# A two-layer hybrid decoder trunk on one core: one plain feed-forward block fewer, zeros set on another engine, and a mended order at the heads

## The chip, the core and the metric

The kernel runs on one core of a Trainium2 chip. Its engines work side by side, each through its own list in order: TensorE (PE; its weight loads are PEld), VectorE (DVE), ScalarE (ACT), GpSimd (POOL), and SyncE (SP), whose queue starts most DMA transfers. The metric is the device time in microseconds (us). Three runs of the kernel before gave a median of 1268.68 us.

## The reference

There are two layers. Each normalises its input, projects it to all heads at once, runs eight forgetting-attention heads and four retention heads, projects their joined outputs back and adds them; then a SwiGLU feed-forward block is added. Sixteen learned tokens stand ahead of the 512 real ones, so layer 0 works on 528 columns.

```
def rmsnorm(x, g):
    y = x32 * lax.rsqrt(jnp.mean(x32 * x32, axis=-1, keepdims=True) + EPS)
...
logit[t,s] = q_t.k_s/sqrt(Dh) + c[t] - c[s], c = cumsum(log f), s <= t     # attention, 8 heads of 64
o_t = sum_{s<=t} gamma_h^(t-s) (q_t.k_s) v_s                               # retention, 4 heads of 128
...
h = h + (silu(x @ w_gate) * (x @ w_up)) @ w_down                           # x: normalised h; 1024 -> 2816 -> 1024
```

## The kernel before

Activations are kept transposed: `h[k]`, k = 0 to 7, holds 128 of the 1024 features over the T = 528 columns. Layer 0 computes all columns in two pieces of 264 (FULL); layer 1 needs the last 512 only (REAL), in one piece.

**Three matmuls for one product.** Each fp32 operand is split into a high part, rounded to the fast matmul's type (`whi`, `xh`, names ending in h or hi), and the rest (`wlo`, `xl`); a product is high times high, high times low, low times high. So each weight tile costs a cast on ScalarE (L199, in the feed-forward's units L900) and a subtraction on VectorE or, in parts of 128, on GpSimd (L202, L901). The same holds for activations (L150 and L151; L327 and L328 for the normalised input). `convert(j)` does it for job j; the job in hand converts the next one's two halves at its second and fifth chunk. `whi` and `wlo` have two buffers.

**Order.** TensorE's order is written out in the program: a list of steps, into which `merge` and `spread` put the steps of the attention heads (`fox_steps`) and the retention heads (`ret_places`) at given positions. The other engines' order is chosen by a scheduler that knows three hints: `high_priority`, `issue_after`, and `pin` (keep in program order). PSUM has four single banks (`psa`) and two double ones (`psd`).

**Attention and retention.** L524 makes a block of logits from the keys with the forget terms (`kc`, built in L467 and L472, and `kx`) and the queries (`qo`, `qs`); L528 masks it and takes the maximum `nmax`, L541 the exponential `pr`; L427 transposes it, and its high and low parts `pth`, `ptl` (L151) go into L586 and L594 against the values. A retention head takes its product in L727, multiplies it by its decay (L732, `sd`), splits it into `rsh` and `rsl`, multiplies by the values in L761 and normalises the head. L664 starts the gate's silu, for heads 0 and 1, with a maximum of x and -80, written as an instruction that takes x twice.

**The feed-forward.** 22 blocks of 128 hidden features go through six rounds, `ROUNDS = ((0, 3), (3, 7), ...)`. A block below PLAIN is plain: gate and up are ordinary products over eight chunks each (96 matmuls of 264 columns in layer 0, 48 of 512 in layer 1), then `u_done` multiplies and splits the result into `ah`, `al`. Any other block is a `Unit`, which makes its two outputs from seven smaller products of half the depth and half the columns, as in fast matrix multiplication: 84 matmuls of 264 columns, in layer 1 of 256. Its parts are a head (first product pair, w1, with the ordinary x), a middle (w2 twice, w3) and a tail (w3, w4). Weights w2, w3, w4 are sums and differences of gate and up weights, formed on VectorE (`make2` to `make4`: L946, L947, L953, L959) and then split: w2 into `fwhi`, `fwlo` from `S` for the first unit of a layer, w3 into `whi`, `wlo` from `fraw`. The x forms (`th`, `tl`, from `S`) are sums of x blocks that `x_forms(0)` to `x_forms(3)` make, inserted every nine steps in the plain blocks. `done` turns a unit's banks into its `ah`, `al`. The products with w_down (`down`, L1047) of a round are put among the units of the next one. The squares for the second norm are summed on VectorE (`ss`, L348), split (`sql`) and summed over partitions by L298.

The final norm's last squares are made in L1140 and summed in L1143 and L1169.

Of the kernel before, what the change touches and what calls it, by code (L numbers as in the profile page):

```python
# [27 lines left out]
PLAIN = 3  # L28
# [11 lines left out]
def hybrid_kernel(ctx, tc, x_t, w_in, w_fl, w_out, w_gate, w_up, w_down, vecs, b_fg, rope, decay, mask, ident, out_t):  # L40
# [42 lines left out]
    def enter_att(l):  # L83
# [37 lines left out]
    def zero(l, t):  # L121
        (nc.gpsimd if l else nc.vector).memset(t, 0.0)  # L122
# [82 lines left out]
    def dense_steps(src, parts, pool=False, banks=False, ahead=(1, 4), own=None, wait=None):  # L205
# [6 lines left out]
        def chunk(k0, k, n, xs, cols, ps, done):  # L212
            def go():
# [77 lines left out]
    def col_rstd(parts, n, cols, rname, pinned=False):  # L291
# [23 lines left out]
    def pin(f, pinned=True):  # L315
        if pinned:
            tc.keep_in_program_order(f)

    def scale_split(st, gcol, cols, then=None):
# [3 lines left out]
        for k in range(NK):  # L323
# [3 lines left out]
            pin(nc.scalar.activation(xh[:, c], h[k][:, c], AF.Copy, scale=g), then)  # L327
# [48 lines left out]
    def forget_gates(l, st):  # L376
# [16 lines left out]
        for ps, (c0, c1) in zip(psf, FULL):  # L393
            with ExitStack() if l else tc.high_priority():
                nc.scalar.copy(z2[:, c0:c1], ps[32:32 + FH, 0:c1 - c0])
# [233 lines left out]
    def ret_dense(l, hd, ly, real, st, which):  # L629
# [23 lines left out]
        def g_done(ps):  # L653
# [3 lines left out]
            if hd > 1:  # L657
                silu(sv(sg, real), LOGS)
# [5 lines left out]
            nc.vector.scalar_tensor_tensor(u, x, -80.0, x, ALU.max, ALU.max)  # L664
# [11 lines left out]
    def ret_steps(l, hd, st, real):  # L676
# [27 lines left out]
        def scores(grp):  # L704
# [87 lines left out]
        def head_norm():  # L792
            d = st["d"]
            r = col_rstd(st["parts"], 128, QC, "r")
# [23 lines left out]
    def out_proj(l, rnd, mix, real):  # L818
# [4 lines left out]
                                rnd == 0 or m2 < 2, rnd == 1 and m2 == 1) for m2 in range(NK // 2)], [])  # L823

    def ffn(l, st, real, last):
# [40 lines left out]
        def x_forms(k):  # L866
            def go():
# [5 lines left out]
                nc.scalar.activation(s[:, 0:2], two(h[k]), AF.Copy, scale=g0)  # L873
# [567 lines left out]
```

## Time and profile before

| | |
|---|---|
| median of three runs | 1268.68 us (1268.33 to 1268.9) |
| profiled execution, its span | 1268.51 us, 1266.7 us |
| granted TensorE clock, mean | 0.998 |
| PE, PEld | 1250.7 us (99%), 1192.2 us (94%) |
| DVE, ACT, POOL | 994.4 us (79%), 706.2 us (56%), 274.3 us (22%) |
| DMA | 116.19 MB, 92 GB/s over the span |
| layer 0's feed-forward, first plain product to first unit | 286.85 to 322.34 us |
| the same in layer 1 | 910.03 to 944.66 us |

In the profile's rows the first number is the start, the second the duration, both in us; then come engine, line, operation, output<-inputs, and xcount where equal neighbours are merged. Square brackets give the idle time before an instruction and who ended it. In rows of waits, the waiting engine and line stand left of the arrow.

### The profile page before, as it was taken

The page shows a single profiled execution, that of the slowest core. Times are in us where ns is not written, and L with a number is a line of the kernel's source. Part 1 is how long each engine was busy: PE and PEld are TensorE (multiplying, and loading weights), DVE is VectorE, ACT ScalarE, POOL GpSimd, SP SyncE. Part 2 cuts the span into 40 slices and gives each one's busy share as a digit, 9 for nine tenths or more (in the row PEclk, how much of TensorE's full clock was granted, in tenths as well). Part 3 has the DMA queues.
Part 4 walks back from the last instruction along what each step waited for, and adds up shares of the span by engine and source line. Part 5 has one row for each costly group of instructions (what it writes and reads, how often), then busy time and mean ns, then how long its engine had stood idle before and what let it go on. Part 6 is the DMA issues. An engine that isn't in the chain of part 4 may idle for free.

```text
span 1266.7 us, 23528 instructions
## 1 busy us (share of the span) xinstructions
PE 1250.7 (99%) x9223; PEld 1192.2 (94%) x9223; DVE 994.4 (79%) x1800; ACT 706.2 (56%) x1305; POOL 274.3 (22%) x540
## 2 busy tenths in 40 slices
PE   9999999999999999999999999999999999999997
PEld 9999999999999999999999989998789999999996
DVE  8887756879988888887786877567899888888867
ACT  7767655676444444444466665557764444444445
POOL 3555546420000000000126556554100000000000
PEclk9999999999999999999999999999999999999999
DMA  6212222223333333332322122222233333333321
GB/s 218 67 60 69 83 76 73 71 67 117 105 97 100 100 101 100 101 101 84 101 77 84 61 84 74 71 89 67 100 96 121 100 101 101 100 101 101 100 84 67
DMA packets 43342, 116.19 MB, mean 92 GB/s; under 512 B 5088, under 2 KB 12000, under 8 KB 43232
## 3 DMA queue, kind: packets, MB, share of 16 engines
q1 hardware_dynamic: 42800, 114.41, 28.1%
q8 instruction: 72, 1.18, 0.4%
q14 instruction: 38, 0.31, 0.1%
q10 hardware_dynamic: 432, 0.29, 0.1%
HBM read 112.58 MB, written 2.10 MB: 91 GB/s over the span
## 4 chain that ended last, share of the span: by engine, by line
PE 91%; DVE 4%; ACT 4%; issue 1%; DMA 0%; ACTq 0%; DVEq 0%
PE psd L225 28%; PE psa L912 18%; PE psd L1047 14%; PE psd L912 13%; PE psa L225 5%; PE psa L1047 4%; PE psa L427 2%; PE psa L524 1%; PE psa L594 1%; PE psa L761 1%; PE psa L727 1%; ACT whi L199 1%; PE psa L298 0%; ACT xh L327 0%; DMA raw<-w_in 0%
## 5 line engine op out<-in xcount | busy, mean ns | idle before, releaser
L202 POOL TENSOR_TENSOR wlo<-raw,whi 128x128 fp32r<-128x128 f32 x504 | 259.1, 548 | 256.0 <-ACT whi L199 235.3
L225 PE MATMUL psd<-xh,whi 128*128 128x264 f32 (+1 forms) x792 | 195.5, 314 | 0.0
L225 PE MATMUL psd<-xh,wlo 128*128 128x264 f32 (+1 forms) x792 | 186.9, 304 | 0.0
L225 PE MATMUL psd<-xl,whi 128*128 128x264 f32 (+1 forms) x792 | 186.4, 303 | 0.4 <-DVE xl L328 0.4
L225 PEld LDWEIGHTS psd<-xh,whi 128*128 128x128 f32 x792 | 128.5, 190 | 4.9 <-ACT whi L199 0.5
L225 PEld LDWEIGHTS psd<-xh,wlo 128*128 128x128 f32 x792 | 127.0, 188 | 6.3 <-DVE wlo L202 0.4
L225 PEld LDWEIGHTS psd<-xl,whi 128*128 128x128 f32 x792 | 127.6, 189 | 5.1 <-DVE xl L328 1.1
L199 ACT CAST whi<-raw 128x512 fp32r<-128x512 f32 (+1 forms) x168 | 97.9, 613 | 41.7 <-PE psd L225 28.6
L900 ACT CAST whi<-raw 128x1024 fp32r<-128x1024 f32 (+2 forms) x62 | 54.8, 885 | 51.2 <-PE psd L912 39.8
L900 ACT CAST fwhi<-raw 128x1024 fp32r<-128x1024 f32 (+2 forms) x62 | 55.6, 897 | 48.0 <-PE psd L912 40.5
L122 POOL MEMSET kc<- 64x528 f32 x2 | 1.1, 532 | 345.4 <-PE psa L912 345.4
L901 DVE TENSOR_TENSOR wlo<-raw,whi 128x1024 fp32r<-128x1024 f32 (+2 forms) x62 | 62.9, 1015 | 12.6 <-ACT whi L900 12.5
L901 DVE TENSOR_TENSOR fwlo<-raw,fwhi 128x1024 fp32r<-128x1024 f32 (+2 forms) x62 | 64.0, 1033 | 11.0 <-ACT fwhi L900 10.7
L912 PE MATMUL psa<-th,whi 128*128 128x264 f32 (+1 forms) x232 | 65.4, 282 | 0.0
L912 PE MATMUL psa<-th,wlo 128*128 128x264 f32 (+1 forms) x232 | 65.4, 282 | 0.0
L912 PE MATMUL psa<-tl,whi 128*128 128x264 f32 (+1 forms) x232 | 65.3, 282 | 0.0
L912 PE MATMUL psa<-th,fwhi 128*128 128x264 f32 (+1 forms) x224 | 63.4, 283 | 0.0
L912 PE MATMUL psa<-tl,fwhi 128*128 128x264 f32 (+1 forms) x224 | 63.3, 283 | 0.0
L912 PE MATMUL psa<-th,fwlo 128*128 128x264 f32 (+1 forms) x224 | 63.2, 282 | 0.0
L541 ACT ACTIVATE pr<-pr,nmax 128x144 f32<-128x144 f32 (+1 forms) x64 | 36.8, 575 | 44.4 <-DVE nmax L528 25.7
L900 ACT CAST fwhi<-S 128x1024 fp32r<-128x1024 f32 x20 | 21.0, 1049 | 68.6 <-PE psa L912 66.5
L978 ACT COPY e<-psa 128x264 f32<-128x264 f32 (+1 forms) x114 | 42.9, 376 | 28.3 <-PE psa L912 24.1
(368 smaller groups left out, 4044.8 us busy)
## 6 DMA issues: line engine op xcount, KB each, us to landing
raw<-w_in SPq DMA_DIRECT2D x54, 512.0 KB, 3.5
raw<-w_gate SPq DMA_DIRECT2D x44, 512.0 KB, 4.0
fraw<-w_up SPq DMA_DIRECT2D x38, 512.0 KB, 3.5
raw<-w_down SPq DMA_DIRECT2D x64, 256.0 KB, 2.9
raw<-w_out SPq DMA_DIRECT2D x16, 512.0 KB, 3.5
raw<-w_down SPq DMA_DIRECT2D x32, 192.0 KB, 2.5
raw<-w_up SPq DMA_DIRECT2D x6, 512.0 KB, 3.5
h<-x_t SPq DMA_DIRECT2D x8, 264.0 KB, 4.5
```

What stands on the lines that cost most here:

```text
L199: pin(nc.scalar.copy(hi, job["raw"][:, c0:c1]), pinned)
L202: pin(sub(lo[:, c:c + step], job["raw"][:, c0 + c:c0 + c + step], hi[:, c:c + step].bitcast(F32)), pinned)
L225: nc.tensor.matmul(ps[1][b][:, 0:c1 - c0], w[:, wk, :], x[:, c0:c1], start=(k == 0 and i == 0), stop=(k == n - 1 and i == 2))
L427: nc.tensor.transpose(ps[:, 128 * j:128 * j + 128], src[:, o:o + 128], idt)
L524: nc.tensor.matmul(sc[0:nq, 0:c1 - c0], qq[:, q0:q0 + nq], kk[:, c0:c1], start=(i == 0), stop=(i == 1))
L541: nc.scalar.activation(pr, pr, AF.Exp, bias=nmax[0:nq], scale=-1.0, accum_out=rsum)
L594: nc.tensor.matmul(po[:, c0:SEQ], v[:, j, :], pp[:, j, META + c0:T], start=(j == 0 and i == 0), stop=(j == 4))
L900: nc.scalar.copy(hi, src)
L901: nc.vector.tensor_sub(lo, src, hi.bitcast(F32))
L912: nc.tensor.matmul(bank()[:, 0:b.shape[-1]], a[:, o + k, :], b, start=(fresh and k == 0 and i == 0), stop=(k == n - 1 and i == 2), skip_gr ...
L978: nc.scalar.copy(self.t["e"][:, i], self.t["x"][:, 0:w])
L1047: nc.tensor.matmul(v[:, 0:c1 - c0], a[:, s * n + k, :], b[:, c0:c1], start=(k == 0 and i == 0), stop=(k == n - 1 and i == 2))
```

## The change

- PLAIN goes from 3 to 2 in both layers: block 2 becomes a unit, still in the first round. With no down products to fill in, its tail follows the next unit's head. The x forms are inserted every seven steps. `whi` and `wlo` get a third buffer, and the gate of block 0 and the last job of the output projection (`far=True`) convert the job after the next one too.
- Layer 0's zeros and ones of the attention's tiles are set on GpSimd.
- The maximum at L664 becomes a `tensor_scalar_max`, with x once.
- In layer 0 the copy of the forget gate's second part is issued after the sum of squares' rounding. The first activation of the x forms in layer 1 is issued after the last xh. Head 2's silu is issued after head 3's last rounding, which has high priority. `rsh` and `rsl` have three buffers. In layer 0 the sums for head 2's norm are copied aside to SBUF, which frees their banks. Some places of the first heads are moved.
- The final norm keeps the square of row 5 as a third tile, so one VectorE sum goes, and the sum over partitions takes four parts, not three.

```diff
-PLAIN = 3
+PLAIN = 2
...
-            (nc.gpsimd if l else nc.vector).memset(q_tiles[s][rest].bitcast(F32), 1.0)
+            nc.gpsimd.memset(q_tiles[s][rest].bitcast(F32), 1.0)
...
-        (nc.gpsimd if l else nc.vector).memset(t, 0.0)
+        nc.gpsimd.memset(t, 0.0)
...
-        return pool.tile([128, NK, 128], F32R, name=tag, tag=tag, bufs=2)
+        return pool.tile([128, NK, 128], F32R, name=tag, tag=tag, bufs=2 if tag[0] == "f" else 3)
...
-                [(NK, *[wp.tile([128, NK, 128], F32R, name=i, tag=i) for i in ("whi", "wlo")])]
+                [(NK, *[wring(i) for i in ("whi", "wlo")])]
...
                 for half, at_step in enumerate(ahead):
                     if k0 + k == at_step:
                         convert(j + 1, 4 * half + 4)
+                        if far:
+                            convert(j + 2, 4 * half + 4)
...
+            if aside:
+                t = tt("sq")
+                for v, (c0, c1) in zip(views, cols):
+                    nc.scalar.copy(t[:, c0:c1], v)
+                views, cols = [t[:, c_all]], [(cols[0][0], cols[-1][1])]
...
-                silu(sv(sg, real), LOGS)
+                with tc.issue_after(other["rounded"]) if hd == 2 else ExitStack():
+                    silu(sv(sg, real), LOGS)
...
-            nc.vector.scalar_tensor_tensor(u, x, -80.0, x, ALU.max, ALU.max)
+            nc.vector.tensor_scalar_max(u, x, -80.0)
...
-            sh = at("rsh", bufs=2)
-            sl = at("rsl", bufs=2)
+            sh = at("rsh", bufs=3)
+            sl = at("rsl", bufs=3)
...
-            split(sh[:, 0:full], sl[:, 0:full], sd[:, 0:full])
+            with tc.high_priority() if hd == RH - 1 and grp[0] == 2 else ExitStack():
+                st["rounded"] = nc.scalar.copy(sh[:, 0:full], sd[:, 0:full]).ins
+                nc.vector.tensor_sub(sl[:, 0:full], sd[:, 0:full], sh[:, 0:full].bitcast(F32))
...
-                                rnd == 0 or m2 < 2, rnd == 1 and m2 == 1) for m2 in range(NK // 2)], [])
+                                rnd == 0 or m2 < 2, rnd == 1 and m2 == 1, far=rnd == 1 and m2 == 3) for m2 in range(NK // 2)], [])
...
-                nc.scalar.activation(s[:, 0:2], two(h[k]), AF.Copy, scale=g0)
+                with tc.issue_after(st["scaled"].ins) if real else ExitStack():
+                    nc.scalar.activation(s[:, 0:2], two(h[k]), AF.Copy, scale=g0)
...
-                    steps += dense_steps(w_gate[l, f], [(0, xs, NK, QC, g_done(f) if f else held.append)], banks=f == 1)
+                    steps += dense_steps(w_gate[l, f], [(0, xs, NK, QC, g_done(f) if f else held.append)], banks=f == 1, far=f == 0)
...
             def after_7():
                 square_b(7)
-                sum_b(5)
                 v = psum_a()[:, 0:nb]
-                sums(v, [fin["one"][0], fin["acc"], fin["one"][1]])
+                sums(v, [fin["one"][0], fin["acc"]] + fin["one"][1:])
...
-            steps.insert(NK + 4 + 9 * i, x_forms(i))
+            steps.insert(NK + 4 + 7 * i, x_forms(i))
...
-            m0, r0, places = (((7 if l else 11, 31 if l else 32.5), (34, 40.5), (13, 33.5, 35.5, 37.5, 39, 40.5, 43, 44, 47.5, 48)),
+            m0, r0, places = (((7 if l else 12, 31 if l else 33), (34, 40.5), (13 if l else 17.5, 33.5, 35.5, 38.3 if l else 38.6, 39, 40.5, 43, 44, 47.5, 48)),
...
-                      ret_places(3, 52, 45.5, 47.5, 57.5, 55.5, 58.5, 60, 64.1, 63, 64.2))
+                      ret_places(3, 52, 45.5, 47.5, 57.5, 54.9, 58.5, 60, 64.1, 63, 64.2))
```

The first place is VectorE in layer 0's first attention block, around the maximum for silu (L664, now L681; `ge<-sg`). Before:

```order
L655 SCALAR_TENSOR_TENSOR sg<-psd,R 128x528
L528 ISA pr,nmax<-psa,msk 128x264
L528 ISA nmax 128x1
L528 ISA pr,nmax<-psa,msk 128x264
L528 ISA nmax 128x1
L664 SCALAR_TENSOR_TENSOR ge<-sg 128x528
L533 TENSOR_TENSOR nmax<-nmax 128x1
L151 TENSOR_TENSOR ptl<-psa,pth 128x128
```

And now:

```order
L544 ISA pr,nmax<-psa,msk 128x264
L544 ISA nmax 128x1
L544 ISA pr,nmax<-psa,msk 128x264
L544 ISA nmax 128x1
L671 SCALAR_TENSOR_TENSOR sg<-psd,R 128x528
L549 TENSOR_TENSOR nmax<-nmax 128x1
L151 TENSOR_TENSOR ptl<-psa,pth 128x128
L681 TENSOR_SCALAR ge<-sg 128x528
```

The maximum has moved behind `nmax` and the `ptl` for which TensorE's L727 waits. The second place is VectorE at the start of layer 0's feed-forward, around the low part of the first unit's w2 (`fwlo<-S`) and w3 (`wlo<-fraw`). Before, with block 3 as the first unit (`al_4467` is block 1's result):

```order
L151 TENSOR_TENSOR al_4467<-tq,ah_4466 128x528
L946 TENSOR_TENSOR S<-fraw 128x512
L151 TENSOR_TENSOR tl_4286<-S,th_4285 128x1056
L848 SCALAR_TENSOR_TENSOR sg<-psd,R 128x528
L901 TENSOR_TENSOR wlo<-raw,whi 128x1024
L947 TENSOR_TENSOR S<-S,raw 128x512
L953 TENSOR_TENSOR fraw<-raw,fraw 128x512
L959 TENSOR_TENSOR raw<-raw,S 128x512
L901 TENSOR_TENSOR fwlo<-S,fwhi 128x1024
L901 TENSOR_TENSOR fwlo<-raw,fwhi 128x768
L856 SCALAR_TENSOR_TENSOR tq<-psd,R 128x528
L901 TENSOR_TENSOR wlo<-fraw,whi 128x1024
```

And now, with block 2 as the first unit (`al_4477` is block 1's result):

```order
L966 TENSOR_TENSOR S<-fraw 128x512
L897 SCALAR_TENSOR_TENSOR S<-h_80,vec,S 128x264
L875 SCALAR_TENSOR_TENSOR tq<-psd,R 128x528
L967 TENSOR_TENSOR S<-S,raw 128x512
L151 TENSOR_TENSOR tl_4290<-S,th_4289 128x1056
L876 TENSOR_TENSOR tq<-tq,sg 128x528
L921 TENSOR_TENSOR fwlo<-S,fwhi 128x1024
L151 TENSOR_TENSOR al_4477<-tq,ah_4476 128x528
L973 TENSOR_TENSOR fraw<-raw,fraw 128x512
L921 TENSOR_TENSOR fwlo<-raw,fwhi 128x1024
L979 TENSOR_TENSOR raw<-raw,S 128x512
L921 TENSOR_TENSOR wlo<-fraw,whi 128x1024
```

Block 1's result and the forms of w3 and w4 have moved behind w2's low part, and the low part of the next unit's w1 (`fwlo<-raw`, 1024) stands ahead of w3's. The third place is a little later on VectorE, at the end of the first unit's `done`; now it reads:

```order
L921 TENSOR_TENSOR wlo<-S,whi 128x1024
L1013 SCALAR_TENSOR_TENSOR tq<-sg,R 128x528
L921 TENSOR_TENSOR fwlo<-raw,fwhi 128x1024
L1001 TENSOR_TENSOR e<-psd,e 128x264
L1015 TENSOR_TENSOR tq<-psa,tq 128x264
L1016 TENSOR_TENSOR tq<-e,tq 128x264
L979 TENSOR_TENSOR raw<-raw,S 128x512
L966 TENSOR_TENSOR S<-fraw 128x512
L151 TENSOR_TENSOR al_4645<-tq,ah_4644 128x528
```

`al_4645` is block 2's result; between the rows shown above and it stand 24 instructions, counted with it, of three units' weight forms and splits. In the kernel before, block 2's result came from a plain block, ahead of the first unit's tail.

More of the change, by code (lines that the diff above doesn't have):

```diff
@@ L203, in convert, with dense_steps @@
             job["split"] = c1
-    def dense_steps(src, parts, pool=False, banks=False, ahead=(1, 4), own=None, wait=None):
+    def dense_steps(src, parts, pool=False, banks=False, ahead=(1, 4), own=None, wait=None, far=False):
         j = len(jobs)
@@ L289, in col_parts, with first_rounding, col_rstd @@
         return sh, sl
-    def col_rstd(parts, n, cols, rname, pinned=False):
+    def first_rounding(st):
+        c = slice(0, T)
+        sh, sl = st["parts"] = tt("sqh", F32R), tt("sql", F32R)
+        st["rounding"] = pin(nc.scalar.copy(sh[:, c], st["acc"][:, c])).ins
+        pin(nc.vector.tensor_sub(sl[:, c], st["acc"][:, c], sh[:, c].bitcast(F32)))
+    def col_rstd(parts, n, cols, rname, pinned=False, aside=False):
         c_all = slice(cols[0][0], cols[-1][1])
@@ L326, in scale_split @@
             g = vcol(gcol + k)
-            pin(nc.scalar.activation(xh[:, c], h[k][:, c], AF.Copy, scale=g), then)
+            st["scaled"] = nc.scalar.activation(xh[:, c], h[k][:, c], AF.Copy, scale=g)
+            pin(st["scaled"], then)
             pin(nc.vector.scalar_tensor_tensor(xl[:, c], h[k][:, c], g, xh[:, c].bitcast(F32),
@@ L394, in forget_gates @@
             with ExitStack() if l else tc.high_priority():
-                nc.scalar.copy(z2[:, c0:c1], ps[32:32 + FH, 0:c1 - c0])
+                with ExitStack() if l else tc.issue_after(st["rounding"]):
+                    nc.scalar.copy(z2[:, c0:c1], ps[32:32 + FH, 0:c1 - c0])
                 nc.vector.tensor_add(z[:, c0:c1], ps[0:FH, 0:c1 - c0], z2[:, c0:c1])
@@ L627, in hybrid_kernel, with ret_dense @@
     KLEN = (128, 128, 128, 128, META)
-    def ret_dense(l, hd, ly, real, st, which):
+    def ret_dense(l, hd, ly, real, st, which, other):
         QC = REAL if real else FULL
@@ L793, in head_norm @@
             d = st["d"]
-            r = col_rstd(st["parts"], 128, QC, "r")
+            r = col_rstd(st["parts"], 128, QC, "r", aside=hd == 2 and not real)
             gn = tmp.tile([128, 1], F32, name="gn", tag="gn")
@@ L1132, in square_b @@
                     t = fft("S", F32, (128, 6, w), 2)
-                    fin["one"] = [t[:, i, 0:nb] for i in range(2)]
+                    fin["one"] = [t[:, i, 0:nb] for i in range(3)]
                     fin["acc"], fin["rb"], fin["tb"] = (t[:, i, 0:nb] for i in range(3, 6))
                     d = fin["acc"]
-                elif m < NK - 2:
+                elif m < NK - 3:
                     fin["sq", m] = d = tt("sq")[:, 0:nb]
                 else:
-                    d = fin["one"][m - NK + 2]
+                    d = fin["one"][m - NK + 3]
                 pin(nc.scalar.activation(d, h[m][:, cb], AF.Square))
```

5 lines of the change are left out of this document (3 added, 2 removed).

## The prediction

> **What bounds the kernel now.** I read the page first, then who waits for whom on TensorE, then the timelines of the two places where the change acts: the first heads of layer 0 and the start of the feed-forward in each layer. From the page, the busy line and the chain of work that ended last:
>
> ```profile
> PE 1250.7 (99%) x9223; PEld 1192.2 (94%) x9223; DVE 994.4 (79%) x1800; ACT 706.2 (56%) x1305; POOL 274.3 (22%) x540
> PE 91%; DVE 4%; ACT 4%; issue 1%; DMA 0%; ACTq 0%; DVEq 0%
> ```
>
> TensorE is the bound, so there are two ways to gain: give it less to do, or take away its waits. These are the waits (us in total, times, longest):
>
> ```profile
> PE psa L727 <- DVE ptl L151: 1.0, 1, 1.0
> PE psa L761 <- DVE rsl L151: 0.9, 3, 0.4
> PE psa L1169 <- ACT S L1140: 0.9, 1, 0.9
> PE psa L524 <- DVE kc L472: 0.8, 1, 0.8
> PE psa L594 <- DVE ptl L151: 0.7, 1, 0.7
> PE psa L524 <- DVE mixt L598: 0.7, 1, 0.7
> PE psa L427 <- DVE sd L732: 0.4, 1, 0.4
> PE psa L524 <- DVE sq L691: 0.4, 1, 0.4
> ```
>
> All but one are waits for VectorE, and the eight are 5.8 us. That caps what mended heads can give. VectorE's 79% is a mean; at the feed-forward's start it is full. Busy time by stage (PE, PEld, DVE, ACT, POOL, then clock and DMA), layer 0 and then layer 1:
>
> ```profile
> 299.00:311.00 12.00, 12.00 (x102) 12.00 (x101) 12.00 (x24) 8.53 (x13) 0.00 (x0) 1.00 0.14 46
> 311.00:322.00 11.00, 11.00 (x94) 11.00 (x93) 11.00 (x16) 5.97 (x8) 0.00 (x0) 1.00 0.26 85
> 933.00:945.00 12.00, 12.00 (x55) 9.78 (x54) 12.00 (x18) 6.89 (x10) 0.00 (x0) 1.00 0.24 78
> ```
>
> There TensorE and VectorE both have no room. Removing TensorE work in front of what VectorE prepares brings the need forward, and the preparation cannot follow for free.
>
> **The blocks, TensorE's side.** In each layer one plain block (gate and up) becomes a unit of seven products. First and last instructions of the stretch up block 1, gate 2, up 2 in each layer (144 and 72 matmuls), then the first unit's head and the first matmul that needs fwlo, the low part of w2:
>
> ```profile
> 304.98 0.28 PE L225 MATMUL psd<-xh,whi 128*128 128x264 f32 x1
> 322.34 0.28 PE L912 MATMUL psa<-xh,whi 128*128 128x264 f32 x1
> 325.49 0.28 PE L912 MATMUL psa<-th,fwlo 128*128 128x264 f32 x1
> ...
> 914.16 0.40 PE L225 MATMUL psd<-xh,whi 128*128 128x512 f32 x1
> 914.95 0.50 PE L225 MATMUL psd<-xl,whi 128*128 128x512 f32 x1 [0.39 <-DVE xl L328]
> ...
> 927.99 0.42 PE L225 MATMUL psd<-xh,whi 128*128 128x512 f32 x1
> 944.66 0.28 PE L912 MATMUL psa<-xh,whi 128*128 128x256 f32 x1
> 947.73 0.28 PE L912 MATMUL psa<-th,fwlo 128*128 128x256 f32 x1
> ```
>
> Layer 0: 17.36/144 = 0.1206 us each; the block's 96 cost 11.57, the unit's 84 cost 10.13: 1.44 saved. Layer 1: 16.67/72 = 0.2315, 48 of them 11.11; 84 of 256 columns at (947.73 - 944.66)/26 = 0.118 are 9.91: 1.20 saved. The wait at 914.95 (about 0.6 with the slower start after it) goes too, since the first activation of x_forms now stands behind the last xh: 0.6. So 3.2 us in all, if VectorE keeps up.
>
> **The blocks, VectorE's side.** From the low part of the squares' sum (sql), VectorE runs without a pause to fwlo and on to the first unit's result (al). Its rows:
>
> ```profile
> 287.27 0.70 DVE L815 TENSOR_TENSOR h<-psd,h 128x528 f32<-128x528 f32 x1
> 291.90 0.70 DVE L151 TENSOR_TENSOR sql<-ss,sqh 128x528 fp32r<-128x528 f32 x1
> 292.52 1.89 DVE L202 TENSOR_TENSOR wlo<-raw,whi 128x512 fp32r<-128x512 f32 x3
> ...
> 320.74 1.23 DVE L901 TENSOR_TENSOR fwlo<-S,fwhi 128x1024 fp32r<-128x1024 f32 x1
> 321.88 0.95 DVE L901 TENSOR_TENSOR fwlo<-raw,fwhi 128x768 fp32r<-128x768 f32 x1
> 322.75 0.70 DVE L856 SCALAR_TENSOR_TENSOR tq<-psd,R 128x528 f32<-128x528 f32 x1
> ...
> 340.54 0.42 DVE L996 TENSOR_TENSOR tq<-e,tq 128x264 f32<-128x264 f32 x1
> 340.88 0.69 DVE L901 TENSOR_TENSOR fwlo<-raw,fwhi 128x512 fp32r<-128x512 f32 x1
> 341.66 0.71 DVE L151 TENSOR_TENSOR al<-tq,ah 128x528 fp32r<-128x528 f32 x1
> ...
> 944.10 1.22 DVE L901 TENSOR_TENSOR fwlo<-S,fwhi 128x1024 fp32r<-128x1024 f32 x1
> ```
>
> Start to start, 512 elements take 0.60, 528 0.62, 768 0.87, 1024 1.14, 264 0.34. In layer 0 fwlo ends at 321.96, 3.5 before its use at 325.49. Now the use comes 11.57 earlier, at 313.92. In the new order of VectorE six conversions fewer stand between sql and fwlo (6 x 0.60; two of them went into idle slots before the output projection, the others belonged to the dropped block), also one sg and one al fewer (2 x 0.62), and fraw and raw now follow fwlo (2 x 0.60): 6.05 less. fwlo ends at 315.9, 2.0 late. Next, wlo of w3: behind fwlo stand al, fraw, a fwlo of 1024 and raw, so it ends at 315.9 + 0.62 + 0.60 + 1.14 + 0.60 + 1.14 = 320.0; TensorE, 24 matmuls after fwlo, wants it at 318.8: 1.2 late. Then unit 2's result, needed as the third chunk of the first down product, since this unit belongs to the first round. Behind w3's wlo the list has 24 instructions up to that al: 4 x 1.14, 0.87, 11 x 0.60, 4 x 0.62 and 4 x 0.34 = 15.9, so 335.9; TensorE does 108 matmuls meanwhile (rest of the middle, the next head, this unit's tail, the next middle, two down chunks), 13.0, and stands at 333.05: 2.8 late. Layer 0: 6.0 lost, 1.44 saved, +4.6.
>
> Layer 1: between sql and fwlo (ends 945.32) six conversions and one sg go, 7 x 0.60 = 4.2; sql starts some 0.4 earlier with ScalarE's new order, and 0.3 of idle goes: 940.4. The use moves from 947.73 by 11.11 + 0.6 to 936.0: 4.4 late. w3's wlo follows at once, in time. Up to al stand 28 instructions, 6 x 1.14 + 0.87 + 17 x 0.60 + 4 x 0.335 = 19.25, so 959.65; TensorE does 118 x 0.118 + 7 x 0.2315 = 15.55 and stands at 955.95: 3.7 late. Layer 1: 8.1 lost, 1.8 saved, +6.3. Feed-forward together: +10.9. Third buffers and early conversions are in these sums: they move two of the six conversions, and no more, ahead of sql. ScalarE's casts for these steps are taken at nothing, since it is busy 6 to 8.5 us of 11 to 12 there.
>
> **The heads, start and tail.** At 62 us VectorE's maximum for silu took 3.72 us, where 528 elements otherwise take 0.62 start to start; eight GpSimd subtractions ran back to back over it, and TensorE waited for the ptl behind it:
>
> ```profile
> 62.32 3.38 POOL L202 TENSOR_TENSOR wlo<-raw,whi 128x128 fp32r<-128x128 f32 x8
> 62.55 3.72 DVE L664 SCALAR_TENSOR_TENSOR ge<-sg 128x528 f32<-128x528 f32 x1
> 66.26 0.28 DVE L151 TENSOR_TENSOR ptl<-psa,pth 128x128 fp32r<-128x128 f32 x1
> ```
>
> Now nmax and ptl stand ahead of it, and it has one input. The waits at L727 (1.0) and L427 (0.4) and half of L761's 0.9: 1.8, the low end 1.0 (only ptl), the high end 2.3. kc: one more dense chunk ahead of it, six matmuls at 0.12 = 0.7 of its 0.8: 0.7 (0 to 0.8). sq at L691: 0.4, its values being placed later. The later L761 waits, with a third rsh and rsl buffer: 0.4. ptl at L594 and mixt at L598, 0.7 each, only indirectly touched: 0.3 each, ends 0 and 0.7. Heads 3.9 (2.5 to 5.3). New costs there: the two copies that set the sums aside (0.4 each on ScalarE, not awaited by TensorE), and silu of head 2 behind a rounding, awaited only by its gate; at nothing, at worst 0.5. For the start and the tail these rows:
>
> ```profile
> 3.71 0.73 ACT L327 ACTIVATE xh<-h,vec 128x528 fp32r<-128x528 f32 x1 [0.28 <-DMA vec<-vecs]
> 5.53 0.73 DVE L328 SCALAR_TENSOR_TENSOR xl<-h,vec,xh 128x528 fp32r<-128x528 f32 x1
> 22.62 1.72 POOL L202 TENSOR_TENSOR wlo<-raw,whi 128x128 fp32r<-128x128 f32 x4 [20.28 <-PE psd L225]
> 1256.98 0.40 DVE L1143 TENSOR_TENSOR S<-S,sq 128x240 f32<-128x240 f32 x1
> ```
>
> Thirteen memsets leave VectorE; the first xl stood behind them, at 5.53, though its xh was there at 4.44. The weights' low parts behind that xl wait for a cast, so of the 1.1 I take 0.4 (0 to 1.1). GpSimd's first conversion comes at 22.6, so the memsets cost it nothing there. In the tail one sum of 0.40 leaves the chain ahead of L1169: 0.4 of the 0.9 (0 to 0.4). Together 4.7.
>
> **Sum.** 1268.51 (span 1266.7 and 1.8 around it) + 4.6 + 6.3 - 4.7 = 1274.7. The profiled execution is 0.17 under the median 1268.68, so about 1274.9; half a microsecond off, since a wait also slows the matmul after it (at 914.95 by 0.1, over nine waits some 0.5 at a guess): 1274.4.
>
> **The rivals.** (1) The lateness stays at w2 and w3 and does not come back at unit 2's result, because VectorE's other work in those 16 to 19 us can wait: losses 3.2 and 4.4, 1268.7 + 3.2 + 4.4 - 3.2 - 4.7 - 0.5 = 1267.9, no change. For it: al in the profile comes 20.0 us after its unit's head and TensorE now wants it after 19.1, so only 0.9 if VectorE is on time. Against: it isn't, and nothing in the list moves al ahead. (2) VectorE is not late at all: 1268.7 - 3.2 - 4.7 - 0.5 = 1260.3, faster. It needs sql 6 earlier in layer 0 and 8 in layer 1, and decides where the 14.1 us of lateness fall under 5.9. Against: the last residual enters at 287.27, when the output projection ends, and from there to sql are 4.6 us, its own slot and six more, in either order. (3) The maximum is starved again. One row speaks against it, a one-input TENSOR_SCALAR amid four back-to-back GpSimd subtractions:
>
> ```profile
> 664.08 3.30 POOL L202 TENSOR_TENSOR wlo<-raw,whi 128x128 fp32r<-128x128 f32 x4
> 665.60 0.58 DVE L472 TENSOR_SCALAR kc<-fs,pick 40x528 fp32r<-40x528 f32 x1
> ```
>
> It took 0.58, and the GpSimd subtractions around it were the ones stretched (3.30 for four, against 3.38 for eight). If the 3.7 us returns, ptl is past already, but sd and rsl wait: 0.8 of the 1.8 lost, 1275.2. The Trainium skill, "SBUF — State Buffer", section "Who interferes with whom", says that tensor_scalar can take the pair of ports shared with GpSimd and that "Issue order, not op shape, decides who blocks"; by that rule the new form could be blocked like the old one. The row above agrees that the two contend, though there GpSimd lost. By the same section a memset, which only writes, does not contend with VectorE's second input, and no row here tests that for the memsets now at the start.
>
> **How the numbers follow.** VectorE late in both layers, as summed: 0.64, with its own range 1270.5 to 1278. Late at w2 and w3 only: 0.15. Starved maximum on top of the sum: 0.09. VectorE not late: 0.12. What a measurement can tell from no change is 0.2%, 2.5 us: below 1266.1 is faster, above 1271.2 slower. Faster: 0.12 and 0.03 of the second case. Slower: 0.59 of the first and 0.09. Same: the rest, 0.17. The range reaches down to the second case's neighbourhood, 1266, and up to 1278: heads at their low end (+2.2) and 1.5 of further waits in ScalarE's casts.
>
> **What would show it.** TensorE waits at the first fwlo matmul of unit 2 (about 2 in layer 0, 4 in layer 1), and at the down product for al of unit 2 (about 3 and 4); VectorE full from 287 to 336. The L727 and L427 waits gone, the maximum under 1 us, the kc wait under 0.2, first xl near 5.2. I am wrong if those two feed-forward waits are missing or under 2 us in all, most likely because VectorE's list could run ahead of the sums in a way these rows don't show.

## The result, and the profile after

The changed kernel takes 1284.47 us, the median of four runs (1283.84 to 1286.47), against 1268.63 for the kernel before. The ratio is 1.0128, with an interval of 1.0113 to 1.0143: slower by 15.8 us. The forecast was slower too, but by 5.7, and the time lies 6.5 above the top of its range. The profiled execution took 1284.48 (span 1282.7), the one before 1268.51 (span 1266.7), so the two traces can be set against each other as they are.

The busy line of the page, and the core's span with its mean granted clock, after:

```profile
PE 1255.3 (98%) x9249; PEld 1198.9 (93%) x9249; DVE 994.3 (78%) x1800; ACT 708.7 (55%) x1313; POOL 286.1 (22%) x552
core 0: 1282.7 us, clock 0.992
```

Before, the core's line read:

```profile
core 0: 1266.7 us, clock 0.998
```

TensorE's busy time went up by 4.6 us, though by the prediction's count the units save it 2.6, and its mean clock fell. The waits of TensorE after (us in total, times, longest):

```profile
PE psd L1067 <- ACT ah L150: 4.2, 1, 4.2
PE psa L932 <- ACT fwhi L920: 4.0, 2, 3.5
PE psa L306 <- ACT sqh L150: 2.1, 1, 2.1
PE psa L932 <- DVE fwlo L921: 2.1, 2, 1.3
PE psa L1067 <- ACT ah L150: 1.8, 1, 1.8
PE psa L1302 <- DVE wide L62: 1.6, 1, 1.6
PE psa L932 <- DVE wlo L921: 0.9, 1, 0.9
PE psa L1067 <- DVE al L151: 0.7, 1, 0.7
PE psa L540 <- ACT whi L199: 0.6, 1, 0.6
PE psa L610 <- DVE ptl L151: 0.5, 1, 0.5
```

Of the eight waits of before only the ptl one (now L610) and the final norm's (not shown, 0.2) are left under their old names; but the product of kc (L540, before L524) still waits 0.6, now for ScalarE. In their place stand waits for the unit's weight forms (L932, fwhi, fwlo and wlo), for unit 2's result at the first down product (L1067), and one that nobody forecast, L306. L1302, at the kernel's start, was 1.6 before too. TensorE's timeline shows where they fall (start, duration, the wait in brackets):

```profile
309.43 0.39 PE L932 MATMUL psa<-th,fwhi 128*128 128x264 f32 x1 [0.49 <-ACT fwhi L920]
311.25 0.39 PE L932 MATMUL psa<-th,fwlo 128*128 128x264 f32 x1 [1.31 <-DVE fwlo L921]
315.35 0.39 PE L932 MATMUL psa<-th,wlo 128*128 128x264 f32 x1 [0.91 <-DVE wlo L921]
330.38 0.51 PE L1067 MATMUL psa<-ah,fwhi 128*128 128x264 f32 x2 [1.83 <-ACT ah L150]
331.54 0.81 PE L1067 MATMUL psa<-al,fwhi 128*128 128x264 f32 x2 [0.65 <-DVE al L151]
...
944.52 0.39 PE L932 MATMUL psa<-th,fwhi 128*128 128x256 f32 x1 [3.53 <-ACT fwhi L920]
945.78 0.58 PE L932 MATMUL psa<-th,fwlo 128*128 128x256 f32 x1 [0.76 <-DVE fwlo L921]
...
966.87 0.79 PE L1067 MATMUL psd<-ah,fwhi 128*128 128x512 f32 x1 [4.18 <-ACT ah L150]
```

Where these rows name ScalarE, it had itself stood idle for VectorE: 1.98 us for `S` ahead of the `fwhi` of 944.52, and 2.19 and 4.44 for `tq` ahead of the `ah` of 330.38 and of 966.87. VectorE shows no idle time between 299 and 332, so layer 0's lateness is its own.

The matmul at 966.87 lasts 0.79, where one of its form otherwise takes 0.40 (the row of e4 below). The stages show why (PE, PEld, DVE, ACT, POOL, then the granted clock and DMA):

```profile
311.30:313.30 2.00, 2.00 (x16) 2.00 (x17) 2.00 (x3) 0.85 (x1) 0.00 (x0) 1.00 0.00 0
332.40:334.40 2.00, 2.00 (x11) 2.00 (x11) 1.37 (x3) 0.00 (x0) 0.00 (x0) 0.50 0.00 0
334.40:336.40 2.00, 2.00 (x18) 2.00 (x18) 0.49 (x1) 0.84 (x1) 0.00 (x0) 0.97 0.04 8
655.50:658.70 3.20, 3.20 (x15) 3.04 (x14) 1.63 (x3) 2.01 (x5) 2.16 (x5) 0.50 0.00 0
945.60:948.80 3.20, 3.02 (x14) 3.02 (x15) 3.20 (x5) 1.66 (x3) 0.00 (x0) 0.50 0.24 58
966.10:972.70 6.60, 5.83 (x23) 5.20 (x24) 2.64 (x5) 1.45 (x2) 0.00 (x0) 0.50 0.00 0
```

After the 1.31 us wait the clock stays at 1.00 and 16 matmuls pass in 2 us; in the row at 332.40, at a clock of 0.50, 11 pass. PE is busy in nearly all of these rows, so no list of waits shows this loss. Four stretches run at half clock, with edges at 331.1 and 334.5, 655.4 and 658.8, 945.5 and 948.9, 966.0 and 972.8. Together they are 17.1 us, so at most half of that, 8.5, can be lost there. Before, the clock is 1.00 from 7.8 us on until TensorE's last matmul:

```profile
7.80:1258.80 1251.00, 1244.38 (x9207) 1187.42 (x9206) 984.64 (x1773) 700.21 (x1294) 272.50 (x530) 1.00 0.28 90
```

The third place is the start of layer 1's attention, on GpSimd and then on ScalarE. GpSimd after:

```profile
643.39 5.74 POOL L202 TENSOR_TENSOR wlo<-raw,whi 128x128 fp32r<-128x128 f32 x8 [385.35 <-ACT whi L199]
...
652.58 0.51 POOL L388 MEMSET mxh<- 128x512 f32 x1
```

ScalarE after, the cast into the tile that GpSimd zeroes and the next instruction:

```profile
653.13 0.22 ACT L150 CAST mxh<-wfr 128x32 fp32r<-128x32 f32 x1 [3.70 <-POOL mxh L388]
653.25 0.63 ACT L150 CAST sqh<-ss 128x528 fp32r<-128x528 f32 x1
```

Before, the same zeros on GpSimd:

```profile
625.81 0.53 POOL L373 MEMSET mxh<- 128x512 f32 x1 [5.96 <-PE psd L1047]
```

Before, layer 1's zeros ran from 616 to 627 us, well ahead of need. Now eight weight conversions stand ahead of them in GpSimd's list; they wait until 643.39 for their casts, and the zeros come behind, in the order written. ScalarE waits 3.70 for mxh, its cast of the sum of squares (sqh) is queued behind, and TensorE, which sums that over partitions at L306, waits 2.1.

From the start of each stage's first matmul in the two traces, the 15.95 us of span come to this. Up to layer 0's feed-forward: 286.85 before, 282.13 now, -4.7. Layer 0's feed-forward, up to its last down product: 357.6 and 364.55, +6.9. From there to layer 1's first matmul of the forget gate: 6.4 and 9.3, +2.9. Layer 1's attention: 259.17 and 259.14, 0.0. Layer 1's feed-forward and the final norm, to TensorE's last matmul: 348.85 and 359.70, +10.85.

### The profile page after: what moved, and what is told of

Same layout as the page of the kernel before. It is cut to its first block, busy times and chain, and to the rows that moved or that the text cites. A ratio compares the mean times of both kernels' runs of the same rounds, so it can differ in the third digit from the quotient of the medians.

```text
span 1282.7 us, 23554 instructions
## 1 busy us (share of the span) xinstructions
PE 1255.3 (98%) x9249; PEld 1198.9 (93%) x9249; DVE 994.3 (78%) x1800; ACT 708.7 (55%) x1313; POOL 286.1 (22%) x552
## 3 DMA queue, kind: packets, MB, share of 16 engines
q1 hardware_dynamic: 42800, 114.41, 27.9%
## 5 line engine op out<-in xcount | busy, mean ns | idle before, releaser
L202 POOL TENSOR_TENSOR wlo<-raw,whi 128x128 fp32r<-128x128 f32 x504 | 267.0, 564 | 594.0 <-ACT whi L199 593.7
L225 PE MATMUL psd<-xh,whi 128*128 128x264 f32 (+1 forms) x744 | 182.5, 314 | 0.0
L225 PE MATMUL psd<-xh,wlo 128*128 128x264 f32 (+1 forms) x744 | 174.0, 302 | 0.0
L225 PE MATMUL psd<-xl,whi 128*128 128x264 f32 (+1 forms) x744 | 173.7, 301 | 0.0
L225 PEld LDWEIGHTS psd<-xh,whi 128*128 128x128 f32 x744 | 120.4, 189 | 4.1 <-ACT whi L199 0.5
L225 PEld LDWEIGHTS psd<-xh,wlo 128*128 128x128 f32 x744 | 119.1, 188 | 5.0
L225 PEld LDWEIGHTS psd<-xl,whi 128*128 128x128 f32 x744 | 119.6, 189 | 3.7 <-DVE xl L343 0.5
L932 PE MATMUL psa<-th,wlo 128*128 128x264 f32 (+1 forms) x248 | 70.9, 286 | 0.9 <-DVE wlo L921 0.9
L932 PE MATMUL psa<-th,whi 128*128 128x264 f32 (+1 forms) x248 | 70.8, 286 | 0.0
L932 PE MATMUL psa<-tl,whi 128*128 128x264 f32 (+1 forms) x248 | 70.7, 285 | 0.0
L932 PE MATMUL psa<-th,fwhi 128*128 128x264 f32 (+1 forms) x232 | 66.3, 286 | 4.0 <-ACT fwhi L920 4.0
L932 PE MATMUL psa<-th,fwlo 128*128 128x264 f32 (+1 forms) x232 | 66.5, 286 | 2.1 <-DVE fwlo L921 2.1
L932 PE MATMUL psa<-tl,fwhi 128*128 128x264 f32 (+1 forms) x232 | 66.1, 285 | 0.0
L1067 PE MATMUL psd<-ah,fwhi 128*128 128x264 f32 (+1 forms) x200 | 57.0, 332 | 4.2 <-ACT ah L150 4.2
```

The costliest lines, as they stand in the source:

```text
L202: pin(sub(lo[:, c:c + step], job["raw"][:, c0 + c:c0 + c + step], hi[:, c:c + step].bitcast(F32)), pinned)
L225: nc.tensor.matmul(ps[1][b][:, 0:c1 - c0], w[:, wk, :], x[:, c0:c1], start=(k == 0 and i == 0), stop=(k == n - 1 and i == 2))
L932: nc.tensor.matmul(bank()[:, 0:b.shape[-1]], a[:, o + k, :], b, start=(fresh and k == 0 and i == 0), stop=(k == n - 1 and i == 2), skip_gr ...
L1067: nc.tensor.matmul(v[:, 0:c1 - c0], a[:, s * n + k, :], b[:, c0:c1], start=(k == 0 and i == 0), stop=(k == n - 1 and i == 2))
```

## The experiments

The theory after the result: VectorE is late for the unit's weight forms, as summed; each long wait then costs TensorE's clock as well; and the third buffers move GpSimd's zeros. The rivals: that the third buffers and not the unit make the feed-forward late; that the lower clock is an accident which costs nothing on the path; that the unit's place in the first round, and not VectorE's room, makes the loss; and, for the heads, that the maximum's form was what helped. The kernel before ran again beside each group of runs, with medians from 1268.63 to 1269.10; ratios are to the runs of the same group.

**e1: the change with three plain blocks.**

```diff
-PLAIN = 2
+PLAIN = 3
```

> The changed kernel with three plain blocks again; everything else of the change stays. Theory A (VectorE late at the first unit, TensorE at half clock after each long wait, and a wait at layer 1's start that the third weight buffers cause): the feed-forward's losses of 6.9 us in layer 0 and 11.5 us in layer 1 go, the 4.2 us at layer 1's start stay, the heads' 6.7 us and the first xl's 0.6 stay gained: about 1265.5 us. Rival 1 (the early conversions and third buffers themselves spoil the feed-forward's start): the losses stay for the most part, 1275 us or more. Rival 2 (the wait at layer 1's start comes from the extra unit, not from the buffers): about 1261.3 us, no wait at L306 near 650 us.

Measured 1265.78, ratio 0.9972 (0.9960 to 0.9983). The longest wait of TensorE:

```profile
PE psa L306 <- ACT sqh L150: 2.1, 1, 2.1
```

No wait at L932 or L1067 is left. Block 2 as a unit thus costs 1284.47 - 1265.78 = 18.7 us, all the loss and more. The L306 wait stays, so it belongs to another part.

**e2: the change with two weight buffers.**

```diff
-        return pool.tile([128, NK, 128], F32R, name=tag, tag=tag, bufs=2 if tag[0] == "f" else 3)
+        return pool.tile([128, NK, 128], F32R, name=tag, tag=tag, bufs=2)
```

> The changed kernel with two buffers for whi and wlo, as before; two plain blocks stay. Theory A: GpSimd again does its last eight conversions for layer 1 behind the setting of zeros, so the wait for sqh (2.1 us) and the slow matmuls behind it go, 4.2 us: about 1280.3 us if the feed-forward's losses stay as they are, and at most 2 us more where two buffers make conversions later. Rival (the buffers are what keeps the feed-forward's losses this low): over 1287 us. Rival 2 of the run before: the wait at layer 1's start stays, about 1284.5 us.

Measured 1279.02, ratio 1.0075 (1.0062 to 1.0088). Its waits:

```profile
PE psa L932 <- ACT fwhi L920: 2.9, 1, 2.9
PE psd L225 <- DVE xl L343: 2.5, 7, 0.7
PE psa L1067 <- ACT ah L150: 2.3, 1, 2.3
```

The L306 wait is gone: it came with the third buffer, with which the conversions stand ahead of the zeros; with two, GpSimd zeroes mxh at 629.70. The unit's waits remain, though in this schedule the 4.2 us wait at layer 1's down product is no longer among the first, and seven small ones for xl are new. The third buffers cost 5.5 us here on balance.

**e3: the mends alone.** The changed kernel with three plain blocks, two buffers, no `far` and the x forms nine steps apart.

```diff
-PLAIN = 2
+PLAIN = 3
...
-        return pool.tile([128, NK, 128], F32R, name=tag, tag=tag, bufs=2 if tag[0] == "f" else 3)
+        return pool.tile([128, NK, 128], F32R, name=tag, tag=tag, bufs=2)
...
-            steps.insert(NK + 4 + 7 * i, x_forms(i))
+            steps.insert(NK + 4 + 9 * i, x_forms(i))
```

> Only the mends outside the feed-forward's blocks: three plain blocks, two buffers, no early conversions, x forms every nine steps. Theory A: the heads give 4.7 us in layer 0 and 1.3 us in layer 1, the tail 0.7, the first xl of layer 1's feed-forward 0.6: 1268.6 - 7.3 = 1261.3 us. Rival (part of that gain came from the early conversions in idle slots): 1263 to 1265 us. Rival (the mends gain nothing of their own): 1268.6 us.

Measured 1261.44, ratio 0.9939 (0.9926 to 0.9953): 7.7 us faster than the kernel before in the same group, and the fastest version of all. All its waits:

```profile
PE psa L1302 <- DVE wide L62: 1.6, 1, 1.6
PE psa L610 <- DVE ptl L151: 0.5, 1, 0.5
PE psa L443 <- DVE nmax L544: 0.2, 1, 0.2
PE psa L1189 <- ACT S L1160: 0.2, 1, 0.2
```

The mends did all they could; the blocks and buffers took back three times that.

**e4: is the clock a cost of its own?** The changed kernel with 30 extra matmuls of 256 columns ahead of unit 2's middle in layer 1, and 15 of 512 ahead of the third chunk of its first down product. They write banks that hold nothing yet, so they fill the waits and change no data.

```diff
+                def warm():
+                    for _ in range(WARM[0] if real and self.f == PLAIN else 0):
+                        nc.tensor.matmul(y()[:, 0:256], ones, st["x"][0][0][:, T - 256:T], start=True, stop=True)
...
+                    if real and f0 == 0 and m == 0 and k == 2:
+                        for _ in range(WARM[1]):
+                            nc.tensor.matmul(t[1], ones, st["x"][0][0][:, T - 512:T], start=True, stop=True)
```

> The changed kernel with unused matmuls that keep TensorE at work in layer 1's two long waits: 30 of 256 columns ahead of the first unit's middle, into a bank that its second product starts afresh, and 15 of 512 columns ahead of the third chunk of the first down product, into an unused bank. Theory A (after a wait of about 2 us or more TensorE runs at half clock for some 3.5 us): the waits end when they did, the clock stays at 1.0, each place saves 1.4 to 1.8 us, 1281.3 us in all. Rival (the slow matmuls behind the waits wait for operands themselves): no change, 1284.5 us, or more by what the unused matmuls take.

Measured 1280.83, ratio 1.0091 (1.0078 to 1.0105), 3.6 under the changed kernel with more work in it. The stages behind the two waits, and the third chunk's first matmul (L1067 is L1074 here):

```profile
945.00:947.00 2.00, 1.65 (x13) 1.65 (x14) 2.00 (x3) 1.61 (x3) 0.00 (x0) 1.00 0.02 4
966.00:968.00 2.00, 2.00 (x19) 2.00 (x19) 0.49 (x2) 0.83 (x1) 0.00 (x0) 1.00 0.00 0
```

```profile
964.55 0.40 PE L1074 MATMUL psd<-ah,fwhi 128*128 128x512 f32 x1
```

The clock stays at 1.00. From layer 1's first feed-forward matmul to TensorE's last the profiled run takes 355.87 us against 359.70: 3.8 saved there. The first wait ends at the same moment: the first matmul with fwlo comes 30.64 us after the feed-forward's start, 30.65 in the changed kernel. So VectorE, not TensorE, sets that end, and the saving lies behind it: the third chunk starts 49.84 after the feed-forward's start against 51.74, and at full clock. The lower clock is a cost on the path, and a separate one. In layer 0, where nothing was filled, this run has the same waits for the result, 1.84 and 0.65, and its clock stays at 1.00 there: see the last section.

**e5: the units' place.** The changed kernel with the first round cut to the two plain blocks.

```diff
-ROUNDS = ((0, 3), (3, 7), (7, 11), (11, 15), (15, 19), (19, 22))
+ROUNDS = ((0, 2), (2, 6), (6, 10), (10, 14), (14, 18), (18, 22))
```

> The changed kernel with rounds ((0, 2), (2, 6), (6, 10), (10, 14), (14, 18), (18, 22)), so that unit 2's result isn't needed until the second round's down products. Theory A (that result's lateness is a wait of its own with half clock behind it): the waits for ah and al and the slow matmuls after them go, 3.1 + 1.4 us in layer 0 and 5.2 + 1.6 us in layer 1; the waits for w2 and w3 and the one at layer 1's start stay: 1284.5 - 11.3 = 1273.2 us. Rival (VectorE is short of time as a whole and the lateness comes back at the next thing it prepares): 1281 us or more.

Measured 1276.65, ratio 1.0060 (1.0048 to 1.0073): between the two forecasts, so neither holds whole. Two of its waits:

```profile
PE psa L932 <- ACT fwhi L920: 4.0, 2, 3.5
PE psd L1067 <- ACT ah L150: 1.4, 1, 1.4
```

The wait for fwhi is unchanged, since VectorE's work ahead of it is. The waits for the result in the first round are gone. But the last round now has four units, and waits for a result came up at the end of each layer, at 622.70 (the 1.4 shown) and 1241.49. A loss was moved in part, and 7.8 us saved; some of those belong to the L306 wait, which is absent here although the conversions stand ahead of the zeros as well. The eight take 4.33 us here, not 5.74, and mxh is zeroed at 648.66, soon enough. So the order alone doesn't make that wait; the lateness of the conversions has a part in it.

**e6: the other way round.** The kernel before with two plain blocks and nothing else.

```diff
-PLAIN = 3
+PLAIN = 2
```

> The kernel before with two plain blocks and nothing else of the change. Theory A: the feed-forward's losses as in the changed kernel, 6.9 and 11.5 us, and two more conversions (1.2 us) ahead of fwlo in each layer, and xl's wait stays (0.6); nothing at layer 1's start: 1268.6 + 6.9 + 11.5 + 2.4 + 0.6 = 1290 us, from 1287 us (early conversions worth nothing) up. Rival (without third buffers VectorE's list comes out in a better order): under 1280 us.

Measured 1288.49, ratio 1.0154 (1.0140 to 1.0168). The size is as expected, the waits are others:

```profile
PE psa L912 <- ACT th L150: 8.2, 2, 4.4
PE psa L912 <- DVE tl L151: 1.6, 2, 0.8
PE psa L912 <- DVE fwlo L901: 1.5, 2, 0.8
```

With the x forms nine steps apart they themselves (th) come too late, and fwlo is hidden behind them. Every seven steps they are in time, and the lateness shows at the weights. VectorE shows no idle time between 299 and 325 here either. So the block's cost is hardly the deadline of one tile; it fits VectorE's room in that stretch.

**e7 and e10: the maximum's form and its place.** e7 is e3 with the old two-input form in the new place; e10 is the kernel before with the new one-input form in the old place.

```diff
-            nc.vector.tensor_scalar_max(u, x, -80.0)
+            nc.vector.scalar_tensor_tensor(u, x, -80.0, x, ALU.max, ALU.max)
```

> As the run with the heads' mends alone, but the maximum again takes x twice, in its new place behind nmax and ptl. Theory A (the two-input form waits for GpSimd's back-to-back subtractions, but what TensorE awaited now stands ahead of it): the maximum takes 2.5 us or more at 62 us, sd and rsl come later, and the time is 0.5 to 1.5 us over the 1261.4 us of the heads alone. Rival (the form never mattered, only the place): the maximum under 1 us, 1261.4 us.

```diff
-            nc.vector.scalar_tensor_tensor(u, x, -80.0, x, ALU.max, ALU.max)
+            nc.vector.tensor_scalar_max(u, x, -80.0)
```

> The kernel before with the one-input maximum in the old place (ahead of nmax and ptl), nothing else changed. Theory F (the form decides: one input isn't shut out by GpSimd's subtractions): the maximum takes about 0.42 us, the waits at L727, L427 and part of L761's go, about 1266.8 us. Theory P (what decides is the moment at which it starts against GpSimd's run, since in the new place the two-input form took only 0.69 us): it takes 3 us or more again, 1268.7 us.

e7 measured 1261.48, ratio 0.9943 (0.9930 to 0.9957), no different from e3. Its maximum and the GpSimd run around it:

```profile
60.31 4.17 POOL L202 TENSOR_TENSOR wlo<-raw,whi 128x128 fp32r<-128x128 f32 x8
61.80 0.69 DVE L681 SCALAR_TENSOR_TENSOR ge<-sg 128x528 f32<-128x528 f32 x1
```

e10 measured 1268.23, ratio 0.9996 (0.9987 to 1.0005), no different from before:

```profile
62.19 3.38 POOL L202 TENSOR_TENSOR wlo<-raw,whi 128x128 fp32r<-128x128 f32 x8
62.41 3.45 DVE L664 TENSOR_SCALAR ge<-sg 128x528 f32<-128x528 f32 x1
```

The form decides nothing. In the old place either form is held up, to 3.45 and 3.72 us; in the new place the old form takes 0.69 and the GpSimd run is the one stretched, 4.17 for eight against 3.38. That agrees with half of the sentence that the prediction quotes from the Trainium skill, "SBUF — State Buffer": op shape doesn't decide who blocks. That issue order does isn't shown. In e10 the max started 0.22 us into the run, in e7 1.49 us into it; what settles it within a run of eight the runs don't show.

**e8: relief on another engine.** The changed kernel with the low parts of up 0, gate 1 and up 1 subtracted on GpSimd.

```diff
-                    steps += dense_steps(w_gate[l, f], [(0, xs, NK, QC, g_done(f) if f else held.append)], banks=f == 1, far=f == 0)
-                    steps += dense_steps(w_up[l, f], [(0, xs, NK, QC, u_done(f))])
+                    steps += dense_steps(w_gate[l, f], [(0, xs, NK, QC, g_done(f) if f else held.append)], f == 1, f == 1, far=f == 0)
+                    steps += dense_steps(w_up[l, f], [(0, xs, NK, QC, u_done(f))], True)
```

> The changed kernel with the low parts of up 0, gate 1 and up 1 made on GpSimd, which is idle in the feed-forward. Theory A (VectorE's number of instructions sets the lateness): four conversions fewer between sql and fwlo, 2.4 us in each layer, so the w2 waits shrink from 2.1 to 0 and from 4.9 to 2.5, with about 1 us of half clock saved: about 1278.5 us. Rival (GpSimd's subtractions and VectorE's two-input instructions shut each other out): VectorE's instructions at 290 to 310 us take longer than 0.70 each, fwlo comes no earlier, 1284.5 us or more.

Measured 1281.22, ratio 1.0097 (1.0084 to 1.0111), 3.3 under the changed kernel. Its longest wait is new:

```profile
PE psd L225 <- DVE sg L867: 5.5, 2, 3.9
```

The new order puts the read of gate 0's sums (sg) later, and TensorE waits for their bank, 3.9 us in layer 0. There the relief brought next to nothing: fwlo starts 27.5 us after the feed-forward's start against 27.9, not the 2.4 earlier that were expected, and the stage takes 364.40 against 364.55. TensorE no longer waits for that fwlo only because it is itself late. Layer 1's feed-forward with the final norm is 3.7 shorter (356.01 against 359.70). Neither forecast holds whole: fwlo came hardly earlier, as the rival said, but the time fell.

**e9: layer 1's gate zeros on VectorE.** The changed kernel, with only mxh's and mxl's zeros moved.

```diff
-            nc.gpsimd.memset(wf.bitcast(F32), 0.0)
+            (nc.vector if l else nc.gpsimd).memset(wf.bitcast(F32), 0.0)
```

> The changed kernel with one thing moved: in layer 1 the zeros of the forget gate's weight tiles (mxh, mxl at L388) are set on VectorE, not on GpSimd. Theory A (with a third buffer GpSimd's eight conversions come ahead of the zeros, the zeros come late, ScalarE's cast into mxh waits for them and the cast of sqh stands behind it): the wait at L306 and the half clock after it go, 4.2 us, about 1280.3 us. Rival (the zeros of kc and qo, still late on GpSimd, hold the same stretch up by another way, or the wait has another cause): 1283 to 1284.5 us.

Measured 1281.61 (1278.07 to 1282.29), ratio 1.0102 (1.0087 to 1.0118). The zeros now:

```profile
647.55 0.48 DVE L388 MEMSET mxh<- 128x512 f32 x1
```

They are there 5 us earlier, and no L306 wait is left. So the zeros' place in GpSimd's list did hold up the sum of squares. The profiled run, 1278.07, is 6.4 under that of the changed kernel, the median only 2.9; the four runs spread over 4.2 us, and in the profiled one layer 0 kept its full clock as well. So the size of this part is known only roughly: 2.9 to 5.5, with e2.

## Why the prediction was wrong

The sign and the first cause were right; the size was not. Against the sum, 1274.7, the trace has 9.75 us more. Two steps carry 9.5 of it; smaller errors nearly cancel.

- **Heads, start and tail, -4.7.** Under-sized by some 1.6. Up to the feed-forward the trace gives 4.7 against 4.3, and the waits for ptl at L727 and for sd at L427 are gone. The 0.7 for kc hardly came: its product waits 0.64 where it waited 0.76. Layer 1's attention, not in the sum, gained 1.3 (259.17 to 259.14 in spite of 1.25 lost to the clock). The final norm's wait is 0.7 shorter, but its sum has two more matmuls of 0.2, so 0.3 is left. e3 has all of this without the blocks, 7.7 in its group; that holds layer 1's xl wait of 0.6 as well.
- **The maximum.** It took 0.41 us, as was forecast, but of the two reasons given the one-input form has no part in it (e7, e10); the place, or the moment of its start, has. The rival of a starved maximum did not come.
- **VectorE's lateness, layer 0, 6.0.** Right, term by term. Counted from matmul start to matmul start, beyond 0.12 for each, TensorE lost 2.3 us at w2 (waits of 0.49 and 1.31; 2.0 forecast), 1.2 at w3 (0.91; 1.2 forecast) and 3.0 at unit 2's result (1.83 and 0.65; 2.8 forecast): 6.5 in all. Counting a list of VectorE's rows from one known end to the next was enough.
- **Layer 1, 8.1.** Right but a little low: 8.9, from 3.7 and 0.9 for the weights (4.4) and 4.3 for the result (3.7). The list for the result was taken as full; VectorE stood idle 1.35 us in it, for a weight:

```profile
962.14 0.69 DVE L967 TENSOR_TENSOR S<-S,raw 128x512 f32<-128x512 f32 x1 [1.35 <-DMA raw<-w_gate]
```

- **The first step that failed: "half a microsecond off, since a wait also slows the matmul after it".** This was taken off for the nine waits that go; the 14.1 us of new waits that the sum itself forecast got no such price. And it is not one matmul that a long wait slows, but all those in a stretch of 3.4 or 6.8 us about and behind its end, at half clock. In layer 0 this is 1.3: in e9 the stage has the same waits at full clock throughout and takes 363.21 us, here 364.55. The 32 matmuls of the forget gate behind the L306 wait take 5.14 instead of 3.89, 1.25. In layer 1 the waits and savings leave 4.0, and filling the two waits gave 3.8 of it back by the stage, 3.6 by the medians (e4). Together some 6.6; another 0.5 in layer 0 stays open. The row at 914.95, from which the term was sized, has a wait of 0.39: too short to show it. The kernel before had no wait from which it could be read, and there the Trainium skill, "TensorE: Matmul & The Clock Gate", bears on it: its table in "What's actually happening" says that the clock halves after an idle window of about 3.4 us and needs as long a busy one to recover. The trace agrees on the recovery (half clock from 331.1 to 334.5) and differs on how idle the window has to be, see below.
- **The second: "Third buffers and early conversions are in these sums", and the memsets at nothing.** The third buffers were followed on VectorE alone. On GpSimd they put eight conversions ahead of layer 1's zeros, and through ScalarE's list that reached TensorE: 2.1 us and 0.2 more at L306, 2.9 by the starts, with the clock 4.2. e2 and e9 each took the wait away. The memsets' new home in layer 0 did cost nothing, but GpSimd's list at layer 1 was never read.
- **The rivals.** Late at w2 and w3 only: no, the result was waited for in both layers; e5 shows that this part is separable. VectorE not late: no.

Without the two failed steps the time would have been about 1284.5 - 6.6 - 2.9 = 1275.0, less than 1 us from the number forecast. That closeness is in part luck: the mends gained 1.6 more than the sum has, and the waits cost 1.3 more, with the open 0.5 beside them.

## What to carry to other kernels

When work is taken from the bounding engine, count the list of the engine that feeds it from a known end to the new deadline; that gave the waits within 1 us here. Then price a long wait twice, the wait itself and the stretch at half clock behind it: in these runs every wait of 2.9 us and more had one behind it, those of 1.4 to 2.3 us only sometimes. And where a ring gets deeper, read the list of every engine that fills it, also where the ring is used next: an early conversion that cannot start yet holds up everything behind it.

## What the runs showed of the hardware

The granted clock fell to 0.50 after much shorter idle times than the 3.4 us that the Trainium skill, "TensorE: Matmul & The Clock Gate", states in "What's actually happening". But the wait's length alone doesn't settle it. After 1.31, 0.91 and (e8, at 932.8) 1.58 us the clock stayed at 1.00; after 1.45 followed by 0.23 (e5, at 622.7), 1.83 followed by 0.65, and 2.12 (L306) it halved. Yet in e9 the same place has waits of 1.82 and 0.65, and the clock stays:

```profile
330.40:332.40 2.00, 1.35 (x9) 1.14 (x10) 1.87 (x4) 0.00 (x0) 0.00 (x0) 1.00 0.00 0
```

And at L306 the changed kernel and e8 both wait 2.12 us; behind it they read, the changed kernel first:

```profile
655.90:657.90 2.00, 2.00 (x10) 1.91 (x9) 0.86 (x1) 1.61 (x4) 1.36 (x3) 0.50 0.00 0
```

```profile
655.90:657.90 2.00, 2.00 (x19) 2.00 (x19) 0.84 (x1) 1.63 (x4) 1.34 (x3) 1.00 0.00 0
```

The edges of the half clock tell more. In the changed kernel it sets in at 331.11, 655.38, 945.51 and 965.99, and lasts 3.4 us or twice that. The distances between these, 324.27, 290.13 and 20.48, are 95, 85 and 6 times 3.413. So the clock of a run seems to be set anew at steps of 3.41 us, by how idle TensorE was in the step before; in other runs the steps lie elsewhere. In the four steps that end at these edges it was idle for 2.1, 2.2, 2.9 and 3.3 us. In e9 an edge, counted back by such steps from 937.67, falls at 330.09 into the wait that ends at 330.37 and splits it, so that no step there is idle for more than 1.6; in e8 one counted back from 963.76 falls at 653.15 into the wait at L306. The same section of the Trainium skill says that the window in which activity is watched runs freely and doesn't start anew with the kernel; the trace agrees. How idle a step must be is known roughly: steps with 2.1 us and more halved the clock in every trace, those with 1.6 and less nearly never, and between them both occurred. Where a wait of some 2 us falls against these steps looks like chance, and in these two places 1.3 to 1.5 us hung on it.

The other surprise is that one VectorE instruction can be held for about 3.4 us by a run of GpSimd subtractions, whether it reads one tile or two (e10), and that the same instruction, once it stands behind nmax and ptl, isn't (e3 0.42 us, e7 0.69).
